# The q and k projections of 15 attention heads by half-size block products, in a stage of their own ahead of the attention

## The chip, the cores and the metric

One core of a Trainium2 chip runs the whole program. The metric is device time in microseconds (us): the median over runs of the same program, here of three. All numbers of the profile come from one further execution that the hardware profiler recorded.

## The reference

A trunk of two layers over 1024 tokens of width 1024, in fp32. The even layer (a gated MLP and a chunkwise mLSTM) and the output products are untouched by the change. The odd layer is differential attention with 16 heads; each head has two queries and two keys of 64 features and a value of 128:

```python
q, k, v, z = jnp.split(h @ w_in, 4, axis=-1)
q = apply_rope(q.reshape(bsz, seq, C_HEADS, 2, C_HEAD_DIM), cos, sin)
k = apply_rope(k.reshape(bsz, seq, C_HEADS, 2, C_HEAD_DIM), cos, sin)
...
p = probs(q1, k1) - lam * probs(q2, k2)          # causal softmax of each
o = rmsnorm(p @ v, subln_g) * (1.0 - lam_init)
o = o.reshape(bsz, seq, C_WIDTH) * jax.nn.silu(z)
return o @ w_out
```

`apply_rope` turns each pair of half-vectors by a position's angle: `[x1*c - x2*s, x1*s + x2*c]`.

## The kernel before, in words

**Products.** Every fp32 matrix product is made of three matmuls on parts. `split2` cuts a tile into a high part (a cast on ScalarE, L96) and the rest (a subtraction on VectorE, L97), and TensorE multiplies high by high, high by low and low by high. The normed tokens lie transposed in two halves of 512 tokens, `hnT[half]` = (`hh`, `hl`), each with 8 blocks of 128 features. One projection unit (`proj_half`, L127 to L135) is 24 matmuls of 128x512 into the PSUM tile `un`: 8 feature blocks by 3 products.

**The odd layer.** `odd_units(h)` (from L406) yields the units of one head: k and q for both halves of the tokens, v (`odd_v`, two units; from `proj_tok`, L150, as 48 matmuls of 256 columns), z for both halves. After each q or k unit comes the rotation: ScalarE copies the unit to `xs` (L437), four DMAs of SyncE fetch it with the quarters swapped into `sw` (L439), VectorE multiplies by the cosines (L440) and the sines (L441) and adds (L442), `split2` makes `xh` and `xl` (L96, L97), and DMAs (L451) copy their halves into the tiles `K` and `Q` from which the attention reads.

**The order.** Head 0's units run first. Then the attention of head h (`odd_head`: scores S L558, masked minimum L563 and exponential L566, probabilities L572, transposes `tp` L590 with a split into `PT`, values L604 and L605, norms L627 and L628) goes in 8 steps, and between them one unit of a later head is issued as fill: in every step for most heads, in the four steps that `SLOTS` names for heads 14 and 15. So 120 units (8 for each of heads 1 to 15) lie beside the attention. Weights are loaded one tile of 128x1024 ahead (`next_w`, `fetch_w` L74) and split when their unit comes. A scheduler may move an instruction ahead of others on its engine; the queues of the engines then run in that order.

```python
left = 8 * (CH - 1)
for h in range(CH):
    att = self.odd_head(odd, h)
    for i in range(NT):
        if i in SLOTS.get(h, range(NT)):
            next(fill, None)
```

GpSimd (POOL) does almost nothing there but issue DMAs; elsewhere it scales rows of `xa` at L344 twice in the program, together with VectorE.

Of the kernel before, what the change touches and what calls it, by code (L numbers as in the profile page):

```python
# [46 lines left out]
class Trunk:  # L47
# [106 lines left out]
    def run(self):  # L154
        tc, nc, io = self.tc, self.nc, self.io
        with tc.tile_pool(name="const", bufs=1) as cp, \
# [41 lines left out]
            self.ahead, self.order = [], [0, 2, 1, 3]  # L198
            for h in range(1, CH):
                half = (h + 1) % 2  # L200
                vs = [h] if h == CH - 1 else [h - half, h - half + 1]
                self.order += [4 * h + 1, 4 * h] + [4 * a + 2 for a in vs] + [4 * h + 3]
# [202 lines left out]
    def odd_units(self, pool, h, ws=None, pss=()):  # L405


        nc, io = self.nc, self.io
        K2, Q2 = [{}, {}], [{}, {}]
        zs = {}  # L410
        self.units[h] = K2, Q2, zs
        ws = ws or [None, None]
# [1 line left out]
        steps = ((1, 0), (0, 0), (0, 1), (1, 1)) if pss else ((1, 0), (1, 1), (0, back), (0, not back))
        for i, (which, half) in enumerate(steps):
            if pss and i == 2:
                run(self.odd_v(pool, h))
            if i >= len(pss) and ws[which] is None:
                ws[which] = self.next_w()
            if back and i == 3:  # L420
                for _ in self.odd_v(pool, h):
                    yield
            for c in range(2):
                if which:
                    K2[c][half] = pool.tile([P, 512], F32R, name=f"K2{c}", tag=f"K2{c}", bufs=4)
                else:
                    Q2[c][half] = [pool.tile([P, 512], F32R, name=f"Q{x}{c}", tag=f"Q{x}{c}", bufs=3 if x == "h" else 2) for x in "hl"]
            hs = slice(half * 512, (half + 1) * 512)
            if i < len(pss):
                ps = pss[i]  # L430
            else:
                ps = self.unit()
                self.proj_half(ws[which], ps, half)

            xs = pool.tile([P, 512], F32, name="xs", tag="xs", bufs=2)
            sw = pool.tile([P, 512], F32, name="sw", tag="sw", bufs=1)
            nc.scalar.copy(out=xs, in_=ps)  # L437
            for a, b in ((0, 32), (32, 0), (64, 96), (96, 64)):
                nc.sync.dma_start(out=sw[a:a + 32], in_=xs[b:b + 32])  # L439
            nc.vector.tensor_tensor(out=xs, in0=xs, in1=self.cos[:, hs], op=ALU.mult)  # L440
# [3 lines left out]
            if which == 0:  # L444
                cp = [(Q2[c][half][i], a, x, c) for i, x in enumerate((xh, xl)) for c in range(2) for a in (0, 64)]
            else:
                cp = [(K2[0][half], 0, xh, 0), (K2[0][half], 64, xl, 0), (K2[1][half], 0, xl, 1), (K2[1][half], 64, xh, 1)]
# [772 lines left out]
```

## Time and profile before

| | |
|---|---|
| median of 3 runs | 2155.84 us (2154.84 to 2157.11) |
| the profiled execution | 2155.46 us |
| its span, from first to last instruction | 2153.7 us |
| TensorE busy | 2122.1 us, 99% |
| VectorE busy | 1375.5 us, 64% |
| ScalarE busy | 943.5 us, 44% |
| GpSimd busy | 188.7 us, 9% |
| mean granted clock of TensorE | 0.997 |

The stretch from about 926 to 1975 us is the attention with its fill; the even layer lies ahead of it and the output product behind. Busy times are of one engine; two engines that work at the same time both count.

### The profile page before, as it was taken

How to read it: one execution, taken by the hardware profiler on the slowest of the kernel's cores; microseconds unless marked ns; L12 is line 12 of the kernel's file. 1: busy time of each engine (PE TensorE's matmuls, PEld its weight loads, DVE VectorE, ACT ScalarE, POOL GpSimd, SP SyncE). 2: the span in 40 equal slices, each digit the busy share in tenths (PEclk: the TensorE clock that was granted, in tenths of full speed). 3: DMA queues.
4: the chain of work that ended last, by engine and by line, in shares of the span. 5: the costliest groups of instructions: out<-in, count | busy, mean ns of one | idle time of the engine just before them, and what ended most of it. 6: DMA issues, size and time to landing. Idle time of an engine off the chain costs nothing.

```text
span 2153.7 us, 33782 instructions
## 1 busy us (share of the span) xinstructions
PE 2122.1 (99%) x12554; PEld 1858.8 (86%) x12554; DVE 1375.5 (64%) x3117; ACT 943.5 (44%) x1907; POOL 188.7 (9%) x315
## 2 busy tenths in 40 slices
PE   8899999999999999999999999999999999998998
PEld 7888889898989889988888888888888888887898
DVE  6352225767677622648777777777877777898525
ACT  5511214343434312335555555555555555665222
POOL 0000000000000000301111111110111011111002
PEclk9999999999999999999999999999999999999999
DMA  4311222111122441255444444444444443336812
GB/s 172 118 40 40 71 87 74 50 64 64 54 70 99 163 170 69 97 144 135 126 111 110 112 112 125 117 109 112 110 112 121 125 108 105 104 85 217 301 50 89
DMA packets 89337, 233.65 MB, mean 108 GB/s; under 512 B 19109, under 2 KB 20037, under 8 KB 89173
## 3 DMA queue, kind: packets, MB, share of 16 engines
q1 hardware_dynamic: 74420, 194.65, 29.7%
q0 software_dynamic: 14752, 36.85, 5.6%
q8 instruction: 99, 1.62, 0.3%
q14 instruction: 66, 0.53, 0.1%
HBM read 136.86 MB, written 27.43 MB: 76 GB/s over the span
## 4 chain that ended last, share of the span: by engine, by line
PE 84%; DVE 5%; DMA 3%; issue 3%; ACT 2%; SPq 2%; POOL 1%; DVEq 0%; POOLq 0%; ACTq 0%
PE un L135 38%; PE wps L295 11%; PE un L150 5%; PE S L558 5%; PE ops L150 4%; PE un L295 3%; PE O L604 3%; PE tp L590 3%; PE xps L135 2%; PE N L941 1%; PE O L605 1%; DMA sw<-xs 1%; PE vps L913 1%; PE dC L941 1%; SPq L451 1%
## 5 line engine op out<-in xcount | busy, mean ns | idle before, releaser
L135 PE MATMUL un<-hh,wh 128*128 128x512 f32 x1240 | 490.2, 395 | 1.2 <-ACT xs L437 1.2
L135 PE MATMUL un<-hh,wl 128*128 128x512 f32 x1240 | 490.2, 396 | 1.0 <-DVE wl L97 0.9
L135 PE MATMUL un<-hl,wh 128*128 128x512 f32 x1240 | 486.9, 393 | 0.0
L97 DVE TENSOR_TENSOR wl<-wr,wh 128x1024 fp32r<-128x1024 f32 (+1 forms) x163 | 205.4, 1261 | 315.2 <-ACT wh L96 283.6
L96 ACT CAST wh<-wr 128x1024 fp32r<-128x1024 f32 (+1 forms) x163 | 170.8, 1049 | 384.5 <-PE un L135 178.0
L135 PEld LDWEIGHTS un<-hh,wl 128*128 128x128 f32 x1240 | 233.0, 188 | 52.2 <-DVE wl L97 3.4
L135 PEld LDWEIGHTS un<-hh,wh 128*128 128x128 f32 x1240 | 233.4, 188 | 46.9 <-ACT xs L437 1.5
L135 PEld LDWEIGHTS un<-hl,wh 128*128 128x128 f32 x1240 | 233.1, 188 | 47.3
L566 ACT ACTIVATE p<-p,mn 128x128 f32<-128x128 f32 (+7 forms) x256 | 197.8, 774 | 122.7 <-DVE mn L563 122.5
L563 DVE CUSTOM_DVE_ANT_0 p<-S,mask 128x128 f32<-128x128 f32 (+7 forms) x256 | 184.9, 751 | 2.2 <-PE tp L590 1.7
L295 PE MATMUL wps<-wh,yh 128*128 128x256 f32 (+1 forms) x576 | 184.2, 321 | 0.2 <-ACT wps L323 0.2
L295 PE MATMUL wps<-wl,yh 128*128 128x256 f32 (+1 forms) x576 | 183.4, 319 | 0.0
L295 PE MATMUL wps<-wh,yl 128*128 128x256 f32 (+1 forms) x576 | 183.4, 319 | 0.0
L150 PE MATMUL un<-wh,hh 128*128 128x256 f32 (+1 forms) x560 | 160.3, 287 | 4.1 <-ACT wh L96 2.6
L150 PE MATMUL un<-wl,hh 128*128 128x256 f32 (+1 forms) x560 | 159.4, 285 | 1.4 <-DVE wl L97 1.4
L150 PE MATMUL un<-wh,hl 128*128 128x256 f32 (+1 forms) x560 | 159.2, 284 | 0.2 <-DVE hl L97 0.2
L97 DVE TENSOR_TENSOR PT<-tp,PT 128x512 fp32r<-128x512 f32 (+1 forms) x192 | 106.1, 553 | 30.4 <-ACT PT L96 30.2
L295 PEld LDWEIGHTS wps<-wh,yh 128*128 128x128 f32 x576 | 109.2, 190 | 9.4 <-ACT wps L323 0.8
L295 PEld LDWEIGHTS wps<-wh,yl 128*128 128x128 f32 x576 | 109.3, 190 | 7.6
L295 PEld LDWEIGHTS wps<-wl,yh 128*128 128x128 f32 x576 | 109.4, 190 | 7.4
L604 PE MATMUL O<-PT,Vh 128*128 128x512 f32 x320 | 113.6, 388 | 0.1
L96 ACT CAST PT<-tp 128x512 fp32r<-128x512 f32 (+1 forms) x192 | 91.6, 477 | 47.4 <-PE tp L590 44.9
(324 smaller groups left out, 4393.5 us busy)
## 6 DMA issues: line engine op xcount, KB each, us to landing
wr<-wO SPq DMA_DIRECT2D x79, 512.0 KB
wr<-wE SPq DMA_DIRECT2D x46, 512.0 KB
sw<-xs SPq DMA_DIRECT2D x256, 64.0 KB
Qh<-xh SPq DMA_DIRECT2D x128, 128.0 KB
Ql<-xl POOLq DMA_DIRECT2D x128, 128.0 KB, 4.0
wr<-wF SPq DMA_DIRECT2D x18, 512.0 KB
wr<-wG SPq DMA_DIRECT2D x18, 512.0 KB
yl<-yd SPq DMA_DIRECT2D x16, 512.0 KB
```

Of the source, the lines that this page charges most:

```text
L96: return (self.nc.scalar.copy(out=out_h, in_=src).ins, self.nc.vector.tensor_tensor(out=out_l, in0=src, in1=out_h.bitcast(F32), op=ALU.sub ...
L97: self.nc.vector.tensor_tensor(out=out_l, in0=src, in1=out_h.bitcast(F32), op=ALU.subtract).ins)
L135: nc.tensor.matmul(out=ps, lhsT=a[:, kb, :], rhs=b[:, kb, :], start=(kb == 0 and i == 0), stop=(kb == KB - 1 and i == 2))
L150: nc.tensor.matmul(out=ps, lhsT=a[:, k0 + k, sl], rhs=b, start=start and k == i == 0, stop=stop and k == n - 1 and i == 2)
L295: self.nc.tensor.matmul(out=ps, lhsT=a[kb][:, sl], rhs=b, start=(kb == 0 and n == 0), stop=(kb == 15 and n == 2))
L451: q.dma_start(out=dst[a:a + 64].bitcast(F32), in_=src[64 * c:64 * c + 64].bitcast(F32))
L558: mm(out=Ss[c][:, lo:lo + n], lhsT=Q2[c][qt // 4][i][:, qs], rhs=K2[c][lo // 512][:, :n], start=i == 0, stop=i == 1)
L563: nc.vector.tensor_tensor_reduce(out=p[:, :W], in0=S[:, :W], in1=self.mask[:, T - W:], scale=-0.125, scalar=1e30, op0=ALU.add, op1=ALU.min ...
L566: nc.scalar.activation(out=p[:, :W], in_=p[:, :W], func=AF.Exp, scale=-1.0, bias=mn, accum_out=s)
L590: self.nc.tensor.transpose(out=tp[:, i, :], in_=p[:, s0:s0 + P], identity=self.ident)
L604: mm(out=O.rearrange("p (a t) -> p a t", a=2)[:, :, a0:], lhsT=Vh, rhs=pt, start=s == 0, stop=False)
L941: mm(out=out, lhsT=lhsT[a], rhs=rhs[b], start=first and i == 0, stop=last and i == 2)
```

## The change

Heads 1 to 15 get q and k in a stage ahead of the attention. q and k of one head are the two row blocks of a 2x2 block product (weights of q and k by two halves of the features; tokens in two halves by the same halves of the features). One level of Strassen's scheme computes it with seven products of half-size blocks, 12 matmuls each, where four units took eight such blocks. The scheme needs four combinations of the token blocks, made once (`make_sums`: sums on VectorE and GpSimd, then split into `T0` to `T3`), and four combinations of each head's weights (`fetch_pair` and `pair`: four GpSimd operations of 128x512). The block results are put together by VectorE reading PSUM. The rotation's cosine product goes to GpSimd, and the rotated and split q and k go to a tensor `qkd` in DRAM. Head 0 keeps its four units. During the attention `odd_load` fetches q and k of the next head by 12 DMAs, `odd_units` has only v and z left (4 units a head), and the fill stands in steps 3, 5, 6, 7.

```diff
-SLOTS = {14: (0, 5, 6, 7), 15: (1, 3, 4, 6)}
+SLOTS = {14: (3, 6), 15: (1, 3, 4, 6)}
+SLOT = (3, 5, 6, 7)
...
+    def make_sums(self, pool):
+        for k in range(4):
+            r = {}
+            for eng, n, half, kb in ((nc.vector, "11", 0, k), (nc.gpsimd, "12", 1, k), (nc.gpsimd, "22", 1, 4 + k), (nc.gpsimd, "21", 0, 4 + k)):
...
+                eng.tensor_tensor(out=r[n], in0=self.hnT[half][0][:, kb, :].bitcast(F32), in1=self.hnT[half][1][:, kb, :].bitcast(F32), op=ALU.add)
...
+            nc.vector.tensor_tensor(out=r["11"], in0=r["12"], in1=r["11"], op=sub)
+            nc.vector.tensor_tensor(out=t2, in0=r["22"], in1=r["11"], op=sub)
+            nc.gpsimd.tensor_tensor(out=r["12"], in0=r["22"], in1=r["12"], op=sub)
+            nc.vector.tensor_tensor(out=r["21"], in0=r["21"], in1=t2, op=sub)
+            for i, x in ((1, t2), (2, r["12"]), (0, r["11"]), (3, r["21"])):
+                self.split2(self.sums[i][0][:, k, :], self.sums[i][1][:, k, :], x)
...
+    def fetch_pair(self, src1, src2):
...
+        x = self.ws.tile([P, 1024], F32, name="wx", tag="wx", bufs=1)
+        (a11, _), (a21, a22) = ((r[:, :512], r[:, 512:]) for r in raw)
+        g = nc.gpsimd.tensor_tensor
+        g(out=x[:, 512:], in0=a11, in1=a21, op=sub)
+        g(out=a21, in0=a21, in1=a22, op=ALU.add)
+        g(out=x[:, :512], in0=a21, in1=a11, op=sub)
...
+    def pair(self, pool, fetched, out):
...
+        a11, a12 = self.split_u(raw1)
+        nc.gpsimd.tensor_tensor(out=raw1[:, 512:], in0=raw1[:, 512:], in1=x[:, :512], op=ALU.subtract)
+        s2, s3 = self.split_u(x)
+        pa = self.unit()
+        self.block_mm(pa, a11, b11, True, True)
...
+        nc.scalar.copy(out=p1, in_=pa)
...
+        self.block_mm(pb, s2, t2, True, True)
...
+        nc.vector.tensor_tensor(out=u2, in0=pb, in1=p1, op=add)
+        self.block_mm(pa, a12, b21, False, True)
+        out(0, 0, pa, None)
+        s1, a22 = self.split_u(raw2)
+        self.block_mm(pb, s3, t3, False, True)
...
+        nc.vector.tensor_tensor(out=u3, in0=pb, in1=p1, op=add)
...
+        self.block_mm(pc, s1, t1, True, True)
+        out(1, 1, pc, u3)
+        s4, = self.split_u(raw1[:, 512:])
+        self.block_mm(pb, a22, t4, False, True)
+        out(1, 0, pb, p1)
+        self.block_mm(pc, s4, b22, False, True)
+        out(0, 1, pc, u2)
...
+    def rope(self, pool, h, which, half, x, y):
...
+        if y is None:
+            nc.scalar.copy(out=xs, in_=x)
+        else:
+            nc.vector.tensor_tensor(out=xs, in0=x, in1=y, op=ALU.add)
+        for a, b in ((0, 32), (32, 0), (64, 96), (96, 64)):
+            nc.sync.dma_start(out=sw[a:a + 32], in_=xs[b:b + 32])
+        nc.gpsimd.tensor_tensor(out=xs, in0=xs, in1=self.cos[:, hs], op=ALU.mult)
+        nc.vector.tensor_tensor(out=sw, in0=sw, in1=self.sin[:, hs], op=ALU.mult)
+        nc.vector.tensor_tensor(out=xs, in0=xs, in1=sw, op=ALU.add)
...
+        self.split2(*parts, xs)
+        for i, t in enumerate(parts):
+            nc.sync.dma_start(out=self.qkd[h, 2 * which + i][:, hs], in_=t.bitcast(F32))
...
-            left = 8 * (CH - 1)
+            left = 4 * (CH - 1)
             for h in range(CH):
+                if h < CH - 1:
+                    self.odd_load(odd, h + 1)
                 att = self.odd_head(odd, h)
                 for i in range(NT):
-                    if i in SLOTS.get(h, range(NT)):
+                    if i in SLOTS.get(h, SLOT):
```

What the change does to the queues is read from the two programs' instruction orders. Names with numbers tell apart tiles of the same name. In GpSimd's queue, in the odd layer, there stood before only DMA issues (`Ql` the low part of a query, `wd` and `msd` results of the attention):

```order
L451 DMA Ql_12924<-xl 64x512 x2
L451 DMA Ql_12926<-xl 64x512 x2
L617 DMA wd_8830<-wt 128x256
L631 DMA msd<-mr 16x1x16
```

Now, for one head's pair of q and k, there stand in a row the four cosine products of head 3 (`xs_9457` to `xs_9564`) and the four weight sums of head 5 (`wr_9580` and `wr_9582` the two raw weight tiles, `wx_9584` their combinations):

```order
L506 TENSOR_TENSOR xs_9457<-xs_9457,cos_8900 128x512
L506 TENSOR_TENSOR xs_9504<-xs_9504,cos_8900 128x512
L506 TENSOR_TENSOR xs_9536<-xs_9536,cos_8900 128x512
L506 TENSOR_TENSOR xs_9564<-xs_9564,cos_8900 128x512
L174 TENSOR_TENSOR wx_9584<-wr_9580,wr_9582 128x512
L175 TENSOR_TENSOR wr_9582<-wr_9582 128x512
L176 TENSOR_TENSOR wx_9584<-wr_9582,wr_9580 128x512
L203 TENSOR_TENSOR wr_9580<-wr_9580,wx_9584 128x512
```

So eight GpSimd operations for each head came in where none was, the last weight sum right ahead of the next cosine products.

VectorE's queue of the same time: the low parts of three weight tiles of head 4 (`wl`, 128x1024 from `wr_9398`, `wr_9400` and `wx_9402`), the block sums that read PSUM (`pb`, `pc`; L503 for head 3, L212 for head 4) and the rotation of head 3:

```order
L98 TENSOR_TENSOR wl_9589<-wr_9398,wh_9588 128x1024
L503 TENSOR_TENSOR xs_9536<-pb_9430,p1_9428 128x512
L98 TENSOR_TENSOR wl_9656<-wr_9400,wh_9655 128x1024
L98 TENSOR_TENSOR wl_9594<-wx_9402,wh_9593 128x1024
L507 TENSOR_TENSOR sw_9458<-sw_9458,sin_8901 128x512
L508 TENSOR_TENSOR xs_9457<-xs_9457,sw_9458 128x512
L98 TENSOR_TENSOR xl_9468<-xs_9457,xh_9467 128x512
L503 TENSOR_TENSOR xs_9564<-pc_9491,u2_9443 128x512
L507 TENSOR_TENSOR sw_9505<-sw_9505,sin_8901 128x512
L212 TENSOR_TENSOR u2_9625<-pb_9612,p1_9610 128x512
L508 TENSOR_TENSOR xs_9504<-xs_9504,sw_9505 128x512
```

The weights' low parts stand together, one behind the other, ahead of the rotation of the results that were ready earlier, and `u2` of head 4 stands behind rotation steps of head 3.

VectorE's queue where the sums of the token blocks end and the first pair begins (`Tl` low parts of the token sums, `r2` and `r21` sums in the making; `wl_9043` is the low part of the first weights of head 1):

```order
L98 TENSOR_TENSOR Tl3_8805<-r21_8884,Th3_8804 128x512
L507 TENSOR_TENSOR sw_8905<-sw_8905,sin_8901 128x512
L507 TENSOR_TENSOR sw_8921<-sw_8921,sin_8901 128x512
L508 TENSOR_TENSOR xs_8904<-xs_8904,sw_8905 128x512
L508 TENSOR_TENSOR xs_8920<-xs_8920,sw_8921 128x512
L98 TENSOR_TENSOR wl_9043<-wr_9026,wh_9042 128x1024
L98 TENSOR_TENSOR xl_8915<-xs_8904,xh_8914 128x512
```

The low part of head 1's first weights comes behind the whole of the sums, 32 VectorE operations, and four steps of head 0's rotation.

## Rows read from the trace of the kernel before

**Rows 1.** The page: busy time of each engine over the span, share, instructions.

```profile
PE 2122.1 (99%) x12554; PEld 1858.8 (86%) x12554; DVE 1375.5 (64%) x3117; ACT 943.5 (44%) x1907; POOL 188.7 (9%) x315
```

**Rows 2.** Waits of TensorE, 925 to 2050 us: us in total, times, longest.

```profile
PE tp L590 <- DVE PT L97: 2.6, 4, 1.9
...
PE tp L590 <- DVE scr L57: 0.2, 1, 0.2
```

**Rows 3.** Three heads' windows: length, busy PE, PEld, DVE, ACT, POOL; clock, DMA share, GB/s.

```profile
1105.10:1169.70 64.60, 64.60 (x374) 56.40 (x373) 49.25 (x108) 35.04 (x79) 8.45 (x16) 1.00 0.43 115
...
sum 193.70, PE 193.70 PEld 169.29 DVE 147.82 ACT 105.28 POOL 25.34; mean PE 64.57 PEld 56.43 DVE 49.27 ACT 35.09 POOL 8.45
```

**Rows 4.** Timeline of TensorE within one unit: start, duration (23 rows between and with these).

```profile
1301.10 0.40 PE L135 MATMUL un<-hl,wh 128*128 128x512 f32 x1
...
1306.11 0.40 PE L135 MATMUL un<-hh,wl 128*128 128x512 f32 x1
```

**Rows 5.** A group of the rotation over the span: busy us, mean ns of one.

```profile
L440 DVE TENSOR_TENSOR xs<-xs,cos 128x512 f32<-128x512 f32 x64 | 44.1, 690 | 37.5 <-DMA sw<-xs 37.4
```

**Rows 6.** Timeline of VectorE, 985 to 1010 us: start, duration.

```profile
985.66 0.68 DVE L440 TENSOR_TENSOR xs<-xs,cos 128x512 f32<-128x512 f32 x1
986.26 0.68 DVE L441 TENSOR_TENSOR sw<-sw,sin 128x512 f32<-128x512 f32 x1
...
998.88 1.22 DVE L97 TENSOR_TENSOR wl<-wr,wh 128x1024 fp32r<-128x1024 f32 x1
1000.01 0.68 DVE L97 TENSOR_TENSOR xl<-xs,xh 128x512 fp32r<-128x512 f32 x1
```

**Rows 7.** GpSimd's L344: ns min/median/max of 16, first and last start.

```profile
L344 POOL TENSOR_TENSOR xa<-xa,gB x16: 1847/1858/2843, 859.3 to 2110.9; 128x768 f32<-128x768 f32 x16
```

**Rows 8.** Timeline of GpSimd, 855 to 885 us: eight operations in a row.

```profile
859.26 16.56 POOL L344 TENSOR_TENSOR xa<-xa,gB 128x768 f32<-128x768 f32 x8 [117.42 <-DMA x2d<-xa]
```

**Rows 9.** Timeline of VectorE beside rows 8.

```profile
862.88 2.96 DVE L97 TENSOR_TENSOR wl<-wr,wh 128x1024 fp32r<-128x1024 f32 x1
871.41 2.69 DVE L97 TENSOR_TENSOR wl<-wr,wh 128x1024 fp32r<-128x1024 f32 x1 [5.58 <-ACT wh L96]
```

**Rows 10.** VectorE with one operand in PSUM, just before rows 8 begin.

```profile
857.02 2.18 DVE L322 TENSOR_TENSOR xa<-wps,xa 128x256 f32<-128x256 f32 x6
```

**Rows 11.** The same line beside L344's second pass on GpSimd (2097.2 to 2112.7).

```profile
2097.95 1.76 DVE L322 TENSOR_TENSOR xa<-wps,xa 128x256 f32<-128x256 f32 x5 [0.30 <-PE wps L295]
```

**Rows 12.** Timeline, 923 to 927 us: the start of head 0's units.

```profile
924.76 1.29 DVE L97 TENSOR_TENSOR hl<-hps,hh 128x512 fp32r<-128x512 f32 x2 [3.69 <-ACT hh L96]
...
925.76 0.50 PE L135 MATMUL un<-hh,wh 128*128 128x512 f32 x1 [1.22 <-ACT xs L437]
```

**Rows 13.** SyncE's queue, 1001 to 1006 us: three DMA issues of the rotation.

```profile
1002.14 1.88 SPq L439 DMA_DIRECT2D sw<-xs  x3
```

**Rows 14.** VectorE's cosine product that waits for them.

```profile
1007.57 0.69 DVE L440 TENSOR_TENSOR xs<-xs,cos 128x512 f32<-128x512 f32 x1 [0.47 <-DMA sw<-xs]
```

**Rows 15.** Windows of the end, columns as in rows 3.

```profile
2143.00:2146.00 3.00, 2.79 (x24) 2.58 (x22) 2.75 (x16) 1.45 (x3) 0.00 (x0) 1.00 0.21 83
2146.00:2149.00 3.00, 0.00 (x0) 0.00 (x0) 2.69 (x15) 1.33 (x3) 0.00 (x0) 1.00 0.50 199
2149.00:2152.00 3.00, 0.00 (x0) 0.00 (x0) 0.60 (x2) 0.93 (x1) 0.00 (x0) 0.63 0.73 291
```

**Rows 16.** Windows of heads 14 and 15, columns as in rows 3.

```profile
1890.00:1910.00 20.00, 19.81 (x101) 16.12 (x99) 18.55 (x47) 10.80 (x24) 3.79 (x8) 1.00 0.32 76
1910.00:1930.00 20.00, 20.00 (x109) 16.59 (x108) 18.59 (x34) 13.54 (x27) 1.46 (x3) 1.00 0.39 109
1930.00:1950.00 20.00, 19.15 (x110) 15.89 (x108) 18.46 (x45) 13.95 (x34) 4.23 (x8) 1.00 0.29 69
1950.00:1970.00 20.00, 16.06 (x76) 12.45 (x76) 18.14 (x41) 12.28 (x29) 1.98 (x4) 0.91 0.88 313
```

More of the change, by code (lines that the diff above doesn't have):

```diff
@@ new lines, in fetch_pair @@
+    def fetch_pair(self, src1, src2):
+        nc, sub = self.nc, ALU.subtract
+        raw = []
+        for s in (src1, src2):
+            self.nfetch += 1
+            r = (self.ws if self.nfetch % 4 >= 2 else self.wp).tile([P, 1056], F32, name="wr", tag="r4", bufs=2)[:, :1024]
+            nc.sync.dma_start(out=r, in_=s)
+            raw.append(r)
+        x = self.ws.tile([P, 1024], F32, name="wx", tag="wx", bufs=1)
[4 more added lines that the diff above has]
+        g(out=x[:, :512], in0=a21, in1=a11, op=sub)
+        return raw[0], raw[1], x
@@ new lines, in split_u, with block_mm @@
+    def split_u(self, raw):
+        self.nsplit += 1
+        last = self.nsplit % 3 == 0
+        n = raw.shape[1]
+        w = [(self.ws if last else self.wp).tile([P, 1024], F32R, name=x, tag=x, bufs=1 if last else 2)[:, :n] for x in ("wh", "wl")]
+        self.split2(*w, raw)
+        return [[y[:, i:i + 512].rearrange("p (k c) -> p k c", k=4) for y in w] for i in range(0, n, 512)]
+    def block_mm(self, ps, w, b, first, last):
+        for k in range(4):
+            for i, (x, y) in enumerate(((0, 0), (0, 1), (1, 0))):
+                self.nc.tensor.matmul(out=ps, lhsT=w[x][:, k, :], rhs=b[y][:, k, :], start=first and k == i == 0,
+                                      stop=k == 3 and i == 2, skip_group_check=True)
@@ L197, in run @@
             self.to_feature(self.xa[6], 6, self.psum, "C", 2)
[L198 to L202, printed above, removed]
+            self.ahead, self.order = [], [0, 1]
             w = [self.next_w(), None]
@@ L403, in odd_setup @@
         self.done = 0
[L405 to L412, printed above, removed]
-        back = h == CH - 1
[L414 to L440, printed above, removed]
-            nc.vector.tensor_tensor(out=sw, in0=sw, in1=self.sin[:, hs], op=ALU.mult)
-            nc.vector.tensor_tensor(out=xs, in0=xs, in1=sw, op=ALU.add)
-            xh, xl = (pool.tile([P, 512], F32R, name=n, tag=n, bufs=b) for n, b in (("xh", 2), ("xl", 1)))
[L444 to L447, printed above, removed]
-            self.split2(xh, xl, xs)
-            for dst, a, src, c in cp:
-                q = nc.gpsimd if src is xl and which == 0 else nc.sync
-                q.dma_start(out=dst[a:a + 64].bitcast(F32), in_=src[64 * c:64 * c + 64].bitcast(F32))
-            yield
-        for _ in () if pss or back else self.odd_v(pool, h):
@@ L454, in odd_units @@
+    def odd_units(self, pool, h):
+        nc = self.nc
+        zs = self.units[h][2]
+        back = h == CH - 1
+        for _ in self.odd_v(pool, h):
             yield
```

79 lines of the change are left out of this document (71 added, 8 removed).

## The prediction

> **What bounds the kernel now.** I read the busy times first [rows 1]: TensorE is busy for 2122.1 of 2153.7 us, every other engine for under two thirds. The list of TensorE's waits over the attention [rows 2] then shows how little it waits: seven kinds of wait, the longest group 2.6 us, the smallest 0.2, together 10.4 us in 1125. The windows of single heads [rows 3] give the stage's numbers: one head takes 64.57 us, TensorE is busy throughout, VectorE for 49.27 (76%), ScalarE for 35.09 (54%). So today the time is the number of matmuls. A change that takes matmuls out gains their spacing, as long as nothing else makes TensorE wait; what follows is mostly about what else.
>
> The sum is made against the profiled execution, 2155.46 us; the median of the runs is 2155.84, 0.38 above. A difference under 0.2% (4.3 us) is about what a measurement of this kernel cannot tell from none.
>
> **1. Matmuls removed.** Within a unit 22 spacings take 1306.11 - 1301.10 = 5.01 us [rows 4], 0.228 each. A half-size block is 12 matmuls, 2.73 us; a head's four units were 8 blocks, 21.9 us, and a pair now is 7 blocks, 19.1 us. 15 heads x 12 x 0.228 = **-41.0 us**. The order of the changed program has the 84 matmuls for each pair, so this term is sure. It is all that the change can gain.
>
> **2. What stands beside a pair.** A unit stood among attention work; a pair stands alone and must be fed from its own 19.1 us. VectorE has 13 operations of 128x512 with both operands in SBUF (sine, addition and low part for four results, one weight sum's low part), 3 of 128x1024 (weights' low parts) and 5 of 128x512 that read PSUM. In a row, 512 columns come every 0.60 us and 1024 every 1.13 [rows 6]; the duration of a single one is 0.69 [rows 5]: 18 x 0.60 + 3 x 1.13 = 14.2 us. That alone would fit. GpSimd gets 8 operations of 128x512, four cosine products and four weight sums. Its 128x768 takes 1.858 us [rows 7]; two thirds of it, 1.24, is my estimate for 512, so 9.9 us. That alone would fit too.
>
> They do not fit beside each other. When GpSimd worked through its eight operations [rows 8], VectorE's 1024-column subtraction took 2.96 and 2.69 us [rows 9] in place of 1.22 [rows 6], 1.74 and 1.47 more, nearly one GpSimd operation each; and one GpSimd operation took 2.843 in place of 1.858 [rows 7], 0.985 more, nearly one VectorE operation. VectorE's additions with one operand in PSUM took 0.36 each before GpSimd began [rows 10] and 0.35 beside it [rows 11]. So two-SBUF operations of VectorE and operations of GpSimd take turns, and PSUM readers are exempt. The turns of one pair add up to 13 x 0.49 + 3 x 0.985 + 9.9 = 19.2 us (GpSimd's delay as the price, half of it for 512) or 13 x 0.60 + 3 x 1.13 + 9.9 = 21.1 us (VectorE's spacing as the price); with the five PSUM readers one after the other, 24.1.
>
> The Trainium skill, "SBUF — State Buffer", section "Who interferes with whom", says that a VectorE instruction with two inputs in SBUF contends with a GpSimd instruction that reads SBUF, and that the shared ports are held exclusively. The trace's 2.96 against 1.22 us agrees. By that rule a pair is bound by the turns; without it TensorE's 19.1 would rule, which is the first rival.
>
> Two in-order queues do not fill such turns without gaps. I walked one steady pair by the order shown ahead. A weight tile's low part waits for the cast (1.05 us) and then for a turn, and in the same stretch GpSimd has its last weight sum and three cosine products queued. `wl_9656` and `wl_9594` each lose about one GpSimd operation, so that the second block's weights come about 2.6 us late. `u2` behind the rotation costs about 0.5, the fourth cosine product with the three weight sums against six VectorE operations about 0.6. Period 19.1 + 3.7 = 22.8 us, between the turns' 19.2 and the 24.1 of everything in a row. 15 x 3.7 = **+55.5 us** (15 x 0.4 = +6 to 15 x 5.9 = +88, a little over the 24.1).
>
> **3. The token sums.** VectorE has 32 two-SBUF operations for them and GpSimd 16, with two cosine products of head 0 among them: 32 x 0.49 + 18 x 1.24 = 38.0 or 32 x 0.60 + 22.3 = 41.5 us of turns; a few of them run earlier, 36 to 39 stay. They cannot end before the last tokens are split, at 926.05 [rows 12]. Then four rotation steps and the first weights' low part follow in VectorE's queue, about 3.5 us: block 1 of head 1 can begin at about 966. TensorE's cover is two units of head 0 from 925.76 [rows 12], 10.9 us, to 936.7. 30 us idle, and about 3 for the first weight combinations, whose memory is that of the sums: **+33 us** (18, if VectorE's 19.2 us ran unhindered, to 45).
>
> **4. The clock after it.** At the end of the program the granted clock is 1.00 in the window in which the last matmuls run and in the next, then 0.63 [rows 15]: of the two levels 1.2 and 2.4 GHz the lower one comes some us after TensorE falls idle. 30 us idle will reach it, and the first blocks run slower: **+3** (0 to one pair's half, 5.5; no row shows how long the return takes). Waits of 2 to 3 us within pairs should leave it alone, as 2146 to 2149 shows.
>
> **5. From pairs to attention.** Head 0's v and z weights stand behind the last rotations, and `K` and `Q` come from DRAM in 12 loads at about 0.63 us of issue [rows 13], landing in some 4 us (last issue 1003.4, use at 1007.57 [rows 14]): **+2** (0 to 10).
>
> **6. The attention itself.** Per head TensorE keeps 64.6 - 21.9 = 42.7 us. VectorE loses 16 rotation and split operations, 16 x 0.69 = 11.0, and two weights' low parts, 2.5: 35.8 us, 84% of the 42.7 where it was 76%. Fill stands in four of eight steps. Nearest rows are heads 14 and 15 of today, which have four units each [rows 16]: from 1890 to 1950 VectorE is at 93% (55.6 of 60) and TensorE at 98.3%, 1.04 us idle; that is 0.74 us in 42.7, and for 15 to 16 heads **+12 us**. Bounds: nothing lost, 0; or 3.2 a head, +48, as 1950 to 1970 loses 3.94 in 20 where fill runs out. SyncE issues 12 loads for a head where it had 32 DMAs (16 swaps, 16 copies), GpSimd 8 fewer; no cost.
>
> Sum: -41.0 + 55.5 + 33 + 3 + 2 + 12 = +64.5, so 2155.46 + 64.5 = **2220 us**, slower by 3%.
>
> **The rivals.**
> *GpSimd's operations fall into VectorE's gaps.* Taking turns costs only where both want the same moment, and VectorE pauses for casts and DMAs; turns at 19.2 would then nearly fit in 19.1. Pairs +6, sums +15 to +18, start of attention +2, attention +6: -41 + 6 + 16 + 2 + 6 = -11, 2144 us, faster. It decides where a pair's period stays under about 20.2 us while the sums leave TensorE idle under 20. Against it: 41 us of turns in the sums with 11 us of cover, and queues in order.
> *The attention runs dry.* With steps 0, 1, 2 and 4 without fill, the chain scores, minimum, exponential, probabilities, transposes is no longer covered, at 84% of VectorE: +48 for +12, 2256 us. For it: the 3.94 us of 1950 to 1970. Against it: 1890 to 1950.
> *SyncE's queue delays the pairs.* 16 swaps, 8 stores and 2 loads for a pair are 26 x 0.63 = 16.4 us of 19.1, in order, and a store waits for its low part with the next swap behind it. If this adds to the turns, the period is 25: +88 for +55.5, 2253 us.
> *Seven blocks are not what TensorE runs.* The instruction order excludes it.
>
> **How the numbers follow.** My forecast's family (pairs 21 to 24 us, sums 22 to 40) 0.56; dry attention 0.12; SyncE 0.10; gaps filled 0.22. The gap rival spans about 2130 to 2160: 0.18 of its chance is faster by over 4.3 us, 0.04 near no change; all the others are slower, so faster 0.18, same 0.04, slower 0.78. The range: 8 in 10 takes in the forecast family, 2175 to 2250, most of the two slow rivals, to 2275, and part of the fast one, from 2148.
>
> **What would show it.** Right: pairs of 22 to 23.5 us, VectorE's 1024-column low parts at over 2 us there, GpSimd's median of 512 columns near 1.24 with longer ones at 1.7 to 1.9; a gap of about 30 us in TensorE before head 1's pair, with a lower granted clock behind it; heads of 43 to 44 us. TensorE's waits would name `wl` from L98 and `u2`. Wrong: pairs under 20 us, or VectorE's two-SBUF operations at 0.69 beside GpSimd's; a gap under 20 us; heads over 45 us; waits on `sw` or on stores of `qkd`.

## The result: 7% slower, outside the range

The changed kernel takes 2309.17 us (median of 4 runs, 2306.12 to 2316.29) where the kernel before takes 2156.28 (median of 4): a ratio of 1.0715, 95% interval 1.0688 to 1.0741. The forecast was 2220 us, with a range of 2148 to 2275. The direction was right, the size was not. The profiled execution of the changed kernel took 2306.12 us, its span is 2304.1: 150.4 more than the span before, where the sum gave 64.5.

The page, as in [rows 1]:

```profile
PE 2153.2 (93%) x12374; PEld 1852.4 (80%) x12374; DVE 1502.3 (65%) x3190; ACT 960.9 (42%) x1923; POOL 341.6 (15%) x327
```

The 180 matmuls are gone (12554 to 12374), and yet TensorE is busy 31 us longer, at 93% of a longer span. So it waits, and part of its work runs slower. Here are TensorE's waits from 925 to 2180 us, the six largest groups (us in total, times, longest), against the 10.4 us in all of [rows 2]:

```profile
PE un L191 <- DVE wl L98: 29.4, 9, 25.2
PE tp L589 <- ACT vt L586: 16.4, 2, 15.0
PE un L191 <- ACT wh L97: 14.0, 8, 2.1
PE pb L191 <- ACT wh L97: 13.3, 13, 2.4
PE pb L191 <- DVE u L212: 11.8, 10, 2.7
PE pc L191 <- ACT wh L97: 9.6, 9, 1.8
```

Two long waits stand at the ends of the pair stage (25.2 and 15.0), the rest are short and many. By stage, in us, with the terms of the sum beside them:

| | forecast | measured | how measured |
|---|---|---|---|
| matmuls removed | -41.0 | -41.0 | 180 fewer |
| token sums, TensorE idle | +33 | +28.9 | 937.3 to 966.66, less two matmuls in it |
| low clock right after | +3 | +4.4 | 22 matmuls at 0.43 us apart in place of 0.228 |
| pairs | +55.5 | +109.1 | 966.66 to 1366.98, less 1258 x 0.228 and less 4.4 |
| pairs to attention | +2 | +15.0 | one wait |
| attention and the rest | +12 | +34 | what remains of 150.4 |

**The token sums.** Where the sums end and the first weights' low part follows, on VectorE and then on TensorE:

```profile
961.18 1.88 DVE L98 TENSOR_TENSOR Tl<-r,Th 128x512 fp32r<-128x512 f32 x3
962.99 1.28 DVE L507 TENSOR_TENSOR sw<-sw,sin 128x512 f32<-128x512 f32 x2
964.19 1.28 DVE L508 TENSOR_TENSOR xs<-xs,sw 128x512 f32<-128x512 f32 x2
965.39 1.21 DVE L98 TENSOR_TENSOR wl<-wr,wh 128x1024 fp32r<-128x1024 f32 x1
```
```profile
966.66 0.80 PE L191 MATMUL un<-hh,wl 128*128 128x512 f32 x1 [25.16 <-DVE wl L98]
```

Block 1 goes on at 966.66; the forecast said about 966. The windows there (columns as in [rows 3]) show VectorE full, GpSimd at 77% beside it, and the granted clock at 0.55 and 0.51 by the time that TensorE resumes:

```profile
940.00:960.00 20.00, 0.73 (x2) 0.30 (x2) 19.94 (x17) 5.37 (x10) 15.33 (x10) 0.55 0.00 0
960.00:980.00 20.00, 10.84 (x24) 7.62 (x25) 11.56 (x15) 5.00 (x7) 12.10 (x9) 0.51 0.49 158
```

**The pairs.** From the first matmul of pair 3 (1018.11) to the last of pair 15 (1366.75) is 348.6 us, so a pair takes 26.8 us in place of 19.1. Matmuls start 0.228 us apart at the full clock. Of the 7.7 us more, 5.3 are spacings over 0.65 us (TensorE waits), 1.8 are spacings of 0.40 to 0.65 us (matmuls at the lower clock), and most of the rest are slower starts of 0.3 to 0.4 us behind a wait. How both arise is seen at the start of pair 11. SyncE, then ScalarE, GpSimd and TensorE:

```profile
1220.16 0.33 SPq L512 DMA_DIRECT2D qkd<-xh  x1
1220.88 0.33 SPq L512 DMA_DIRECT2D qkd<-xl  x1
1221.30 0.90 SPq L169 DMA_DIRECT2D wr<-wO  x2
```
```profile
1225.20 1.04 ACT L97 CAST wh<-wr 128x1024 fp32r<-128x1024 f32 x1 [1.22 <-DMA wr<-wO]
1232.22 1.04 ACT L97 CAST wh<-wx 128x1024 fp32r<-128x1024 f32 x1 [0.30 <-POOL wx L176]
```
```profile
1228.20 1.29 POOL L174 TENSOR_TENSOR wx<-wr 128x512 f32<-128x512 f32 x1 [6.21 <-DMA wr<-wO]
```
```profile
1226.30 0.50 PE L191 MATMUL un<-hh,wh 128*128 128x512 f32 x1 [1.56 <-ACT wh L97]
1231.97 0.56 PE L191 MATMUL pc<-Th,wh 128*128 128x512 f32 x1 [1.84 <-ACT wh L97]
1233.32 0.80 PE L191 MATMUL pb<-Th,wh 128*128 128x512 f32 x1 [0.79 <-ACT wh L97]
1233.91 0.63 PE L191 MATMUL pb<-Tl,wh 128*128 128x512 f32 x1
1234.34 0.63 PE L191 MATMUL pc<-Tl,wh 128*128 128x512 f32 x1
```

The two weight loads are issued at 1221.30, behind the stores of a result whose low part has just been made. What needs them starts 4 and 7 us later; the weight combinations, their casts and low parts follow only then, and TensorE waits for the casts. From 1233.32 on the matmuls come 0.43 us apart. The granted clock of the same stretch:

```profile
1226.00:1231.00 5.00, 3.30 (x12) 2.10 (x12) 1.22 (x1) 0.38 (x2) 2.65 (x3) 1.00 0.58 168
1231.00:1234.00 3.00, 1.24 (x3) 0.78 (x4) 2.02 (x2) 2.44 (x3) 2.92 (x2) 0.71 0.20 44
1234.00:1240.00 6.00, 6.00 (x18) 4.68 (x17) 5.17 (x4) 0.62 (x1) 4.31 (x3) 0.58 0.00 0
```

The operations of VectorE and GpSimd in the pairs (993 to 1366 us, grouped by line; mean ns of one) took turns, but less often than foreseen. The sine product has a mean of 1032 ns where it took 0.68 us, the 1024-column low part 1427 and 1648 where it took 1.22 [rows 6]. The block sums that read PSUM (L503) kept 690 ns:

```profile
L506 POOL TENSOR_TENSOR xs<-xs,cos 128x512 f32<-128x512 f32 x55 | 90.4, 1649 | 141.8 <-DMA sw<-xs 129.8 <-DVE xs L508 4.7 <-DVE xl L98 4.6
L507 DVE TENSOR_TENSOR sw<-sw,sin 128x512 f32<-128x512 f32 x56 | 57.8, 1032 | 3.7 <-DMA sw<-xs 3.7
L98 DVE TENSOR_TENSOR wl<-wr,wh 128x1024 fp32r<-128x1024 f32 x28 | 40.0, 1427 | 30.4 <-ACT wh L97 30.4
L98 DVE TENSOR_TENSOR wl<-wx,wh 128x1024 fp32r<-128x1024 f32 x14 | 23.1, 1648 | 20.2 <-ACT wh L97 20.0
L503 DVE TENSOR_TENSOR xs<-pc,u 128x512 f32<-128x512 f32 x28 | 19.3, 690 | 1.5
L174 POOL TENSOR_TENSOR wx<-wr 128x512 f32<-128x512 f32 x13 | 20.6, 1586 | 54.8 <-DMA wr<-wO 54.8
```

More than half of the sine products were not lengthened at all. Over all heads (min/median/max of 64, in ns):

```profile
L507 DVE TENSOR_TENSOR sw<-sw,sin x64: 678/692/1814, 963.0 to 1384.1; 128x512 f32<-128x512 f32 x64
```

And GpSimd itself mostly waited: 129.8 us for the swaps, which read the tile that the cosine product overwrites, and 54.8 for weight loads. Both are DMAs of SyncE's queue. That speaks for the SyncE rival beside the turns, and the experiments had to tell them apart.

**The way to the attention.** TensorE's wait, and ScalarE's copy that ends it:

```profile
1390.27 1.12 PE L589 MATMUL tp<-ident,vt 128*128 128x128 f32 x4 [14.97 <-ACT vt L586]
```
```profile
1385.68 0.62 ACT L97 CAST xh<-xs 128x512 fp32r<-128x512 f32 x1 [2.72 <-DVE xs L508]
1388.68 1.04 ACT L97 CAST wh<-wr 128x1024 fp32r<-128x1024 f32 x1 [1.44 <-DMA wr<-wO]
1389.63 1.07 ACT L586 COPY vt<-un 128x512 f32<-128x512 f32 x2
```

Head 0's value projection was computed early, from 1367 on, but its copy stands in ScalarE's queue behind the casts of the last rotations, which drain until 1386, and then behind two weight casts, the second of which waits 1.44 us for its load.

**The attention.** One head (columns as in [rows 3]):

```profile
1535.40:1579.40 44.00, 43.88 (x278) 39.15 (x277) 36.58 (x91) 28.39 (x69) 4.29 (x9) 1.00 0.47 120
```

44.0 us, VectorE at 83%, no wait of a matmul that the list would name, but 1.3 us more than 42.7. TensorE's weight loads name a part of it. Those of the scores wait for the masked minimum for 1.6 us in some 14 heads before (1000 to 1900 us) and for 8.0 us in some 14 heads after (1440 to 2060 us), which is 0.46 us a head more:

```profile
PEld S L558 <- DVE mn L563: 1.6, 3, 1.2
```
```profile
PEld S L670 <- DVE mn L675: 8.0, 31, 0.5
```

The last two heads lose more. In the 60 us up to the attention's last transposes TensorE was busy for 55.2 us before (1908 to 1968 us) and is busy for 48.2 after (2062 to 2122 us), beside a VectorE that is busy for 56.7:

```profile
sum 60.00, PE 55.21 PEld 45.02 DVE 54.58 ACT 40.66 POOL 8.45; mean PE 18.40 PEld 15.01 DVE 18.19 ACT 13.55 POOL 2.82
```
```profile
sum 60.00, PE 48.15 PEld 37.11 DVE 56.71 ACT 41.33 POOL 4.93; mean PE 16.05 PEld 12.37 DVE 18.90 ACT 13.78 POOL 1.65
```

### The profile page after: what moved, and what is told of

It reads as the page before. It is cut to its first block, busy times and chain, and to the rows that moved or that the text cites. A ratio compares the mean times of both kernels' runs of the same rounds, so it can differ in the third digit from the quotient of the medians.

```text
span 2304.1 us, 33655 instructions
## 1 busy us (share of the span) xinstructions
PE 2153.2 (93%) x12374; PEld 1852.4 (80%) x12374; DVE 1502.3 (65%) x3190; ACT 960.9 (42%) x1923; POOL 341.6 (15%) x327
## 4 chain that ended last, share of the span: by engine, by line
PE 71%; DVE 10%; issue 6%; DMA 6%; ACT 4%; POOL 3%; SPq 1%; DVEq 0%; POOLq 0%; ACTq 0%
PE un L136 22%; PE wps L417 10%; PE un L240 7%; PE S L670 6%; PE ops L240 4%; PE un L417 3%; PE O L716 3%; PE tp L702 3%; DMA wr<-wO 2%; PE xps L136 2%; PE pb L191 2%; DVE xl L98 2%; PE N L1053 1%; PE O L717 1%; DVE xs L508 1%
## 5 line engine op out<-in xcount | busy, mean ns | idle before, releaser
L98 DVE TENSOR_TENSOR wl<-wr,wh 128x1024 fp32r<-128x1024 f32 (+1 forms) x178 | 219.9, 1236 | 324.9 <-ACT wh L97 298.3
L136 PE MATMUL un<-hh,wh 128*128 128x512 f32 x760 | 303.3, 399 | 1.2 <-ACT xs L501 1.2
L136 PE MATMUL un<-hh,wl 128*128 128x512 f32 x760 | 300.3, 396 | 0.0
L136 PE MATMUL un<-hl,wh 128*128 128x512 f32 x760 | 300.1, 395 | 0.0
L136 PEld LDWEIGHTS un<-hh,wh 128*128 128x128 f32 x760 | 143.8, 189 | 30.9 <-ACT xs L501 1.5
L136 PEld LDWEIGHTS un<-hh,wl 128*128 128x128 f32 x760 | 143.3, 189 | 31.2
L136 PEld LDWEIGHTS un<-hl,wh 128*128 128x128 f32 x760 | 143.6, 189 | 29.5
L97 ACT CAST xh<-xs 128x512 fp32r<-128x512 f32 x64 | 39.7, 621 | 214.3 <-DVE xs L508 164.3
L506 POOL TENSOR_TENSOR xs<-xs,cos 128x512 f32<-128x512 f32 x64 | 103.6, 1624 | 158.2 <-DMA sw<-xs 144.6
L670 PE MATMUL S<-K,Qh 128*128 128x512 f32 (+3 forms) x384 | 111.9, 366 | 4.8 <-DVE mn L675 3.2
```

The costliest lines, as they stand in the source:

```text
L97: return (self.nc.scalar.copy(out=out_h, in_=src).ins, self.nc.vector.tensor_tensor(out=out_l, in0=src, in1=out_h.bitcast(F32), op=ALU.sub ...
L98: self.nc.vector.tensor_tensor(out=out_l, in0=src, in1=out_h.bitcast(F32), op=ALU.subtract).ins)
L136: nc.tensor.matmul(out=ps, lhsT=a[:, kb, :], rhs=b[:, kb, :], start=(kb == 0 and i == 0), stop=(kb == KB - 1 and i == 2))
L506: nc.gpsimd.tensor_tensor(out=xs, in0=xs, in1=self.cos[:, hs], op=ALU.mult)
L670: mm(out=Ss[c][:, lo:lo + n], lhsT=Q2[c][i][:, qs], rhs=K2[c][:, lo:lo + n], start=i == 0, stop=i == 1)
```

## The experiments

All totals below are of one execution each, beside one of the kernel before on the same chip (2154.0 to 2159.7). The four runs of the changed kernel lie 10 us apart, and two kernels whose pair stage is that of the changed kernel (the last two below) take 26.7 and 27.2 us a pair: smaller differences show nothing. A pair's period is taken as above, from pair 3 to pair 15. The edits are against the changed kernel; `...` marks lines left out.

### Is it the turns or the queue?

**Without the swaps.**

```diff
-        for a, b in ((0, 32), (32, 0), (64, 96), (96, 64)):
-            nc.sync.dma_start(out=sw[a:a + 32], in_=xs[b:b + 32])
-        nc.gpsimd.tensor_tensor(out=xs, in0=xs, in1=self.cos[:, hs], op=ALU.mult)
-        nc.vector.tensor_tensor(out=sw, in0=sw, in1=self.sin[:, hs], op=ALU.mult)
+        nc.vector.tensor_tensor(out=sw, in0=xs, in1=self.sin[:, hs], op=ALU.mult)
+        nc.gpsimd.tensor_tensor(out=xs, in0=xs, in1=self.cos[:, hs], op=ALU.mult)
```

> Leaves out the swap of the quarters: the sine product is taken of the unswapped tile, so the 16 swap DMAs of each pair are gone; all operations of VectorE and GpSimd stay. Queue theory (SyncE's queue, in order, with swaps, stores and weight loads behind one another, is what stretches a pair from 19.1 to 26.7 us): pairs fall to 21 to 23 us, total 2235 to 2255. Turns theory (VectorE's two-SBUF operations and GpSimd's exclude each other): those operations are all still there, pairs stay at 25 to 27 us, total 2290 to 2310.

Measured: 2253.2 us, 23.9 us a pair. Between the two forecasts: 2.9 of 7.7 us go with the DMAs, 4.8 stay without them. What stays is one regular wait, 42.0 us in 14 pairs:

```profile
PE pb L191 <- DVE u L212: 42.0, 14, 3.3
```

**Cosine products on VectorE** (`nc.gpsimd` to `nc.vector` in `rope`).

> The four cosine products of a pair go from GpSimd to VectorE; every DMA stays. Turns theory: 4 x 1.28 us of GpSimd's turns become 4 x 0.60 of VectorE, a pair falls by 2 to 3 us to about 24, total 2265 to 2275. Queue theory: the queue is unchanged, pairs stay at 26 to 28 us, total 2295 to 2325.

Measured: 2261.48 us, 24.6 us a pair, as the turns theory said: four operations more on VectorE make the stage 2.2 us a pair faster. Nothing is left out here. But the edit also takes the cosine products, and with them GpSimd's waits for swaps, from ahead of the weight sums in GpSimd's queue, which neither forecast priced; how much of the 2.2 us is turns is not shown.

**Both.**

```diff
...
+        nc.vector.tensor_tensor(out=sw, in0=xs, in1=self.sin[:, hs], op=ALU.mult)
+        nc.vector.tensor_tensor(out=xs, in0=xs, in1=self.cos[:, hs], op=ALU.mult)
```

> Both at once: no swap DMAs (the sine product is taken of the unswapped tile, so the rotation is left wrong) and the cosine products on VectorE, which leaves GpSimd its four weight sums a pair. If the two causes add (26.8 - 2.9 for the swaps - 2.2 for the cosine), pairs of 21 to 22 us, total 2215 to 2225; if both removals shorten one and the same chain, the rotation that PSUM readers of VectorE's queue stand behind, 19.5 to 20.5 us or the same 23.5 to 24 as with one of them.

Measured: 2208.56 us, 20.8 us a pair: 6.0 less, where the single edits give 2.9 and 2.2. That is more than their sum. VectorE is now busy for 195.97 of 200 us (1060 to 1260), close to a limit itself:

```profile
1060.00:1260.00 200.00, 184.01 (x800) 149.15 (x800) 195.97 (x239) 66.48 (x95) 65.98 (x39) 1.00 0.43 150
```

**No operation of GpSimd.**

```diff
...
-        g(out=x[:, 512:], in0=a11, in1=a21, op=sub)
-        g(out=a21, in0=a21, in1=a22, op=ALU.add)
-        g(out=x[:, :512], in0=a21, in1=a11, op=sub)
-        return raw[0], raw[1], x
+        return raw[0], raw[1], raw[0]
...
-        nc.gpsimd.tensor_tensor(out=raw1[:, 512:], in0=raw1[:, 512:], in1=x[:, :512], op=ALU.subtract)
...
+        nc.vector.tensor_tensor(out=xs, in0=xs, in1=self.cos[:, hs], op=ALU.mult)
```

> No operation of GpSimd in a pair: cosine products on VectorE, and the weight sums are left out (the first raw tile stands for the combinations; casts and splits stay). All swaps and stores stay on SyncE's queue. Turns theory: without GpSimd no turns, and no combination that waits for both loads: 19.5 to 21 us a pair. Queue theory: swaps, stores and loads still delay each other, 23.5 to 25 us as with the cosine on VectorE alone.

Measured: 2230.46 us, 22.6 us a pair. Between the two again: 4.3 us of the 7.7 go with GpSimd's work (and with the combinations' wait for both loads), 3.4 are left where no turns are.

**No rotation at all.** The two products, the addition and the swaps are taken out of `rope`; the copy or sum, the split and the stores stay.

> The rotation is left out (no swap, no cosine, sine or addition); block results are split and stored as they are, the weight sums stay on GpSimd. If the rotation is what the pairs' PSUM readers and weight splits are held up by, pairs fall to TensorE's 19.1 to 20 us, total 2180 to 2195. If the seven products hold themselves up (weight loads, weight sums, two banks that are read between accumulations), 21.5 us or more remains, total over 2215.

Measured: 2177.16 us and 19.04 us a pair. In the two windows of this kernel from 1000 to 1200 us TensorE is never idle, and GpSimd still does its weight sums, with every weight load in the same queue behind the stores:

```profile
1000.00:1100.00 100.00, 100.00 (x443) 82.81 (x442) 61.19 (x69) 37.10 (x52) 34.82 (x21) 1.00 0.49 167
1100.00:1200.00 100.00, 100.00 (x442) 82.80 (x442) 62.78 (x71) 38.54 (x54) 36.38 (x22) 1.00 0.49 167
```

The seven products feed themselves. None of the 7.7 us is left without the rotation beside them.

**The rotation beside plain products.** Heads 1 to 15 in the same stage, by four units of 24 matmuls.

```diff
...
-                self.pair(qk, cur, lambda i, j, x, y: self.rope(qk, h, i, j, x, y))
+                for which in (1, 0):
+                    u = self.next_w()
+                    for half in range(2):
+                        pu = self.unit()
+                        self.proj_half(u, pu, half)
+                        self.rope(qk, h, which, half, pu, None)
```

> The stage ahead of the attention without the seven products: each of heads 1 to 15 gets its four units of 24 matmuls there, with the same rotation, the same stores and the same token sums (which nothing uses now). TensorE needs 21.9 us for a head. Turns theory: GpSimd has four operations for a head in place of eight and no block sum reads PSUM, so a head takes 22 to 23 us. Queue theory: the 26 DMAs of a head stand in the same queue with the same rotation between them, a head takes 25 us or more, little less than a pair's 26.7.

Measured: 2242.8 us, and a head takes 23.0 us, where its matmuls alone take 21.9 (96 matmuls from 994.2 to 1316.8 us, 14 heads); in 330 us from 975 on TensorE is busy for 324.2. Its waits from 970 to 1300 us, with all the swaps, stores and loads of the changed kernel:

```profile
PE un L136 <- ACT xs L505: 2.9, 11, 0.3
PE un L136 <- ACT wh L97: 1.6, 4, 0.7
PE un L136 <- DVE wl L98: 0.3, 1, 0.3
```

So the turns theory's 22 to 23 us just hold here, and the queue theory's 25 falls in that form: the same DMAs in one queue allow 23.0. The plain stage, with more matmuls, is 66 us faster than the seven products.

### Where in the queue?

**Swaps from ScalarE's queue** (`nc.sync` to `nc.scalar` for the four swaps in `rope`).

> The 16 swap DMAs of a pair are issued from ScalarE's queue, the stores and the weight loads stay on SyncE's. Queue theory: weight loads no longer stand behind swaps, pairs fall to 21 to 24 us (24 if ScalarE's own casts now stand behind swaps), total 2235 to 2275. Turns theory: nothing changes in the turns, pairs stay at 25 to 27 us, total 2290 to 2315.

Measured: 2351.19 us, 30.7 us a pair, worse than any forecast. TensorE's one large wait there is on ScalarE's casts of weights, which now stand behind swaps that wait for their data (from 993 to 1421 us):

```profile
PE pb L191 <- ACT wh L97: 109.5, 14, 8.7
```

**Weight loads from ScalarE's queue** (`nc.sync` to `nc.scalar` in `fetch_pair`).

> The changed kernel with the pairs' weight loads issued from ScalarE's queue, nothing else. GpSimd waits 61 us in all for these loads. If they are late because they stand behind swaps and stores on SyncE and this is the queue's price, pairs fall to 23 to 25 us. If the price is the swaps' and stores' own, 26 to 27.5 us.

Measured: 2290.35 us, 25.4 us a pair: 1.4 us less, between the two forecasts. The waits moved to ScalarE's copy of the first block, behind its new DMA issues:

```profile
PE un L191 <- ACT p L208: 55.8, 12, 6.0
```

**Stores from GpSimd's queue** (`nc.sync` to `nc.gpsimd` for `qkd` in `rope`), the cosine products left where they are.

> The changed kernel with the stores on GpSimd's queue, the cosine products left on GpSimd: the queue's part alone. With both edits a pair took 21.7 us, with the cosine edit alone 24.6. If the two add, 26.8 - 2.9 = about 24 us, total 2260 to 2270. If stores now hold up the cosine products on GpSimd's queue, 26 us or more.

Measured: 2274.49 us, 25.1 us a pair, 1.7 less, between the two forecasts. The single large wait is again on `u`:

```profile
PE pb L191 <- DVE u L212: 50.9, 14, 5.2
```

**Stores from GpSimd's queue and cosine products on VectorE.**

> Nothing left out: cosine products on VectorE and the eight stores of a pair issued from GpSimd's queue, so SyncE has the swaps and loads alone. Queue theory: swaps no longer wait behind stores, a pair falls from 24.6 to 21 to 23 us, total 2210 to 2240. Rival: GpSimd's weight sums now stand behind stores that wait for the rotation, the combinations come later, 25 us or more, total over 2265.

Measured: 2218.3 us (before: 2154.0), 21.7 us a pair. The queue theory's range. The two edits give 1.7 and 2.2 us alone and 5.1 together.

**More tiles for the rotation.**

```diff
-        self.cos = pool.tile([P, T], F32, name="cos")
-        self.sin = pool.tile([P, T], F32, name="sin")
+        self.sin = self.cos = pool.tile([P, T], F32, name="sin")
...
-        xs = pool.tile([P, 512], F32, name="xs", tag="xs", bufs=3)
-        sw = pool.tile([P, 512], F32, name="sw", tag="sw", bufs=2)
+        xs = pool.tile([P, 512], F32, name="xs", tag="xs", bufs=4)
+        sw = pool.tile([P, 512], F32, name="sw", tag="sw", bufs=3)
```

> The changed kernel with one more tile each for xs (4) and sw (3). To make room the cosine table is left out and the sine table stands in its place; all operations and DMAs stay. If a pair is stretched because the rotations of its four results follow one another through too few tiles (a swap waits for a free sw, and stores and loads stand behind it on SyncE), pairs fall from 26.8 to 23 to 25 us, total 2250 to 2285. If the rate of turns or of DMA issues stretches it, 26 to 27 us, total 2295 to 2315.

Measured: 2314.66 us, 26.5 us a pair. One tile more of each is not it; still more tiles were not tried.

**PSUM banks that need not be read in between.**

```diff
-        pb = bank("pb")
+        bank4 = lambda: self.psum.tile([P, 512], F32, name="pb", tag="pb", bufs=4)
+        pb = bank4()
...
-        self.block_mm(pb, s3, t3, False, True)
+        pb = bank4()
+        self.block_mm(pb, s3, t3, True, True)
...
-        nc.vector.tensor_tensor(out=u3, in0=pb, in1=p1, op=add)
+        nc.vector.tensor_tensor(out=u3, in0=pb, in1=u2, op=add)
...
-        self.block_mm(pb, a22, t4, False, True)
-        out(1, 0, pb, p1)
+        pb = bank4()
+        self.block_mm(pb, a22, t4, True, True)
+        out(1, 0, pb, u3)
```

> The changed kernel with one edit: the second, fourth and sixth block each get a PSUM bank of their own (four in turn), and the sums are carried in SBUF (u3 from u2, the last from u3), so that TensorE need not wait for VectorE's reading of a bank before it accumulates on. Same number of operations, DMAs and turns. Theory (what stops TensorE is chiefly that a PSUM reader stands in VectorE's queue behind rotation steps that wait for a swap or a turn): pairs fall from 26.8 to 23 to 25 us, the waits on u vanish, those on weights' casts, which stand behind the rotation's casts, stay. Rival (the throughput of turns and queue): 26 to 27 us, the waits only change their names.

Measured: 2304.49 us, 26.6 us a pair. The waits on `u` are gone and stand elsewhere:

```profile
PE pc L191 <- DVE xs L506: 24.4, 13, 5.1
PE un L191 <- ACT wh L97: 19.5, 8, 3.4
```

The theory that the reading of PSUM in VectorE's queue is the cause falls: it is where the delay shows, not where it comes from.

**The banks with stores on GpSimd's queue and cosine on VectorE.**

> The same banks with the cosine products on VectorE and the stores on GpSimd's queue. There 24.4 us of 14 pairs' waits were on u. If only the reading order is left as a cause: 19.1 to 20 us a pair, total 2185 to 2195. If VectorE's own load (16.6 us of 19.1, in order) holds: 20.5 to 21.7 us, total 2205 to 2220.

Measured: 2216.7 us, 21.3 us a pair: VectorE's own load, or its order, holds, as with `pb` before now with `pc` (20.8 us of waits).

### The other two terms

**Cover for the token sums**, on top of the last kernel:

```diff
-            self.ahead, self.order = [], [0, 1]
+            self.ahead, self.order = [], [0, 1, 5, 4]
...
+            for which in (1, 0):
+                w1 = self.next_w()
+                for half in range(2):
+                    p1u = self.unit()
+                    self.proj_half(w1, p1u, half)
+                    self.rope(qk, 1, which, half, p1u, None)
             tp.release()
...
```

> As the kernel with banks and stores on GpSimd's queue, and head 1's q and k by four units of 24 matmuls placed ahead of the pairs, as cover for the token sums, in place of head 1's pair. If the 24 to 30 us in which TensorE idles there are only a lack of ready matmuls, 10 to 18 us less than without; if the units wait for xs tiles, whose rotation stands behind the sums in VectorE's queue, 0 to 5 us less.

Measured: 2210.27 us, 6.4 less, which is within what two runs of one kernel can differ. The gap is still there, for a reason that neither case named: the units' own weights are split behind the sums in VectorE's queue.

```profile
964.57 0.80 PE L136 MATMUL un<-hh,wl 128*128 128x512 f32 x1 [23.02 <-DVE wl L98]
```

**Fill of the attention in later steps** (`SLOT` of 4, 5, 6, 7).

> The changed kernel with fill in steps 4 to 7 of the attention in place of 3, 5, 6, 7. If the attention loses 1.3 to 1.5 us a head because steps without fill run dry, a fourth dry step in a row costs more: heads of 44.8 us or more, total over 2320. If it loses it to VectorE's share, wherever the fill stands, heads stay at 43.8 to 44.2 and the total at 2303 to 2318.

Measured: 2309.66 us, heads of 44.2 us. Dry steps are not what the heads lose by.

**Less work for VectorE in the attention.**

```diff
-            nc.vector.scalar_tensor_tensor(out=z, in0=z, scalar=1.0, in1=ps, op0=ALU.add, op1=ALU.mult)
...
-        nc.vector.scalar_tensor_tensor(out=wt, in0=wt, scalar=self.gain,
-                                       in1=st["zs"][j // 2][:, (j % 2) * 256:(j % 2 + 1) * 256], op0=ALU.mult, op1=ALU.mult)
```

> The changed kernel without the SiLU's last product and without the product of the attention's result with gain and z: VectorE does 3.3 us a head less, both off the chain from scores to values. If VectorE's share makes the heads 44.0 us in place of 42.4, they fall to 42.6 to 43.3 us, total 2285 to 2300. If it is the chain within a head, 43.8 to 44.1, total 2303 to 2315.

Measured: 2303.68 us, heads of 44.1 us, though VectorE fell from 36.6 to 34.2 us a head:

```profile
1535.00:1579.00 44.00, 43.76 (x277) 38.85 (x277) 34.20 (x84) 28.26 (x69) 4.13 (x9) 1.00 0.46 120
```

VectorE's share is not it either. What makes a head 44.0 in place of 42.7 us stays open in the main: a chain within the head is left of the two theories, and the score weights' wait for the masked minimum, 0.46 us a head more than before, is a piece of it. TensorE counts as busy for 43.9 of the 44.0, so the rest is spread over small delays that the profile does not name.

## Why the prediction was right and wrong

**Right, point by point.** Term 1 holds: 180 matmuls fewer, and 19.04 us a pair where nothing else makes TensorE wait. Term 3 is right in mechanism and nearly in size: block 1 at 966.66 against about 966, 28.9 us against 33. Term 4's first part holds: the clock is at the lower of its two levels (1.2 GHz) after the long gap, 4.4 us against 3. The turns, on which term 2 rested, are there: the sine product's mean is 1032 against 680 ns, the cosine product's 1649 against 1290 undisturbed, and the block sums from PSUM are exempt. The Trainium skill, "SBUF — State Buffer", section "Who interferes with whom", says that a VectorE instruction with two inputs in SBUF contends with a GpSimd instruction that reads SBUF, under an exclusive lock; the trace agrees, with those 1032 against 680 ns. But turns were rarer than forecast: the 1024-column low parts were to take over 2 us and have means of 1.43 and 1.65, and the median sine product took 692 ns. So a good part did fall into VectorE's pauses, as the gap rival had it; that rival is out by its own signs, which asked for periods under 20.2 us and an idle stretch under 20. Without GpSimd's operations a pair is 4.3 us shorter, near the 3.7 that the turns were forecast to cost, but that run also drops the wait for both weight loads, so the nearness may be luck.

**Wrong: "Period 19.1 + 3.7 = 22.8 us".** It is 26.8. The step that failed is that the SyncE rival was set beside the turns as another way, with 0.10, where both hold at once. The path of a result is copy or sum, four swap issues, landing, a cosine product that must wait for the swaps, addition, cast, low part, store. It passes the in-order queues of four engines, some of them twice. A turn lost on VectorE delays a store; the store delays the swaps and the weight loads behind it on SyncE; the loads delay GpSimd's sums and the casts. That is the argument; shown are its ends: without the rotation 19.0 us, plain products with the rotation 23.0 nearly without waits, GpSimd's work or the swaps taken away 22.6 and 23.9, and two edits of 1.7 and 2.2 us that give 5.1 together. Gains above their sum would also come from two limits side by side, of which the longer one rules; whether the two causes lengthen each other or bind side by side is not shown. The rival's price of 25 us was itself too low by 1.8, though its issues were priced too high: a store took 0.33 us and not 0.63.

**Wrong: "Waits of 2 to 3 us within pairs should leave it alone".** That sentence was read from one gap after unbroken work [rows 15]. In the pairs such gaps recur, and the granted clock falls to 0.58 after one of them. Matmuls at the lower clock make up 1.8 us a pair, 26 us in pairs 2 to 15, about half of what term 2 missed (54 us). How much of it TensorE would have spent waiting at the full clock is not shown. In the kernels with fewer waits it is less: nothing with neither swaps nor cosine products on GpSimd (granted clock 1.00), 0.6 us a pair with stores on GpSimd's queue and the cosine on VectorE.

**Wrong: term 5, from pairs to attention, +2.** It is 15.0. The step named weights behind the last rotations, but not ScalarE's copy of the values behind all of these casts, and not how far the rotations lag behind TensorE: some 19 us, as long as a pair. The two kernels with stores on GpSimd's queue and cosine on VectorE wait 6 us there.

**Too small: the attention's 12 us.** 34 with all that remains, 20 of it 15 heads at 1.3. Heads 14 and 15 of the kernel before gave 0.74 us a head, too little; the cause is open in the main, as told above. Of the other 14 us, 7 are in the last two heads, where TensorE is idle for 11.9 of 60 us and not 4.8. There head 14 has two units of fill in place of four, so the dry attention, a rival with 0.12, is in part true at that place.

No version beats the kernel before. With everything that the rotation costs taken away, which leaves the result undone, the total is still 2177.2 against 2154.0: the sums' gap and the attention's loss are larger than the 41 us.

## What to carry to other kernels

Work that runs as fill has its latency hidden by what it fills between; moved into a stage of its own, every queue that its results pass through in order is on the path, so follow one result and one weight tile through all queues and count what stands ahead of them, DMAs with the rest. Two causes that can hold at once are no alternatives: give them a price together. Here taking both away gained more than the sum of what each gave alone. Before a scheme that saves a few per cent of matmuls, price the stage that feeds it with the feeding's own operations left out and in; here 41 us were to gain and 190 were given back.
